# Two heads in one generator: the chunk solves of a hybrid trunk's mixer, run pair by pair on compact 32x32 blocks

## The chip, the cores and the metric

One core of a Trainium2 chip runs the whole kernel in one launch. The metric is device time in microseconds (us), the median over runs. The engines are named as in the profile: PE (TensorE, matmuls), PEld (its weight loads), DVE (VectorE), ACT (ScalarE), POOL (GpSimd) and SP (SyncE, which issues DMAs).

## What is computed

A trunk of two layers on one sequence of 512 tokens and 1024 channels. Each layer is a gated feed-forward, a mixer and a second feed-forward, each between two RMS norms. The mixer is the place of the change:

```
proj = h @ w_in            # q, k, v, z of 4 heads of 128; beta, a; u (512 channels of S5)
q, k, v = silu(causal_dwconv(qkv));  q, k normalised per token
per head, in chunks:       # gated delta rule
    lmat   = (k * beta) k^T * decay, strictly lower
    sol    = solve(I + lmat, [v * beta | k * beta * exp(g)])
    attn   = q k^T * decay
    S, o   = recurrence over the chunks with sol, attn and the state S
y_gdn = rms_norm(o) * silu(z)
y_s5  = S5 (a diagonal state-space scan) on u, with a gated output
y     = [y_gdn | y_s5] @ w_out
```

The triangular solve is the part that the change rewrites. The kernel works with chunks of 128 tokens, so that each head has four systems of 128x128, and it computes each system's inverse X: first all diagonal blocks of 16x16 by substitution on DVE, then levels that join two inverted blocks by matmuls (16 to 32, 32 to 64, 64 to 128).

## The kernel before

Projections and feed-forwards are matmuls of 128x512 in pieces, each product as three matmuls of high and low parts (mm3, L266 to L270). For them ACT casts each weight tile to its high part wh (L225), and DVE or, for the mixer's weights, POOL takes the low part wl (L233).

The mixer of a layer is built from generators, Python functions that record instructions up to a `yield`. The loop at its end calls every active generator once a round, and beside them some steps of the main work: nine a round in `main1` (projections of head 2, of the S5 input u and of head 3, by ORDER = "2u3"; heads 0 and 1 are projected ahead), one or two in `main2` (z, the S5 gate gl, the output projection od). Of the instructions so recorded a scheduler sets each engine's order; from then on an engine runs its queue strictly in that order, and waits on semaphores at its head.

`gen_head` (L921) is the generator of one head. Four of them exist; heads 0 and 1 start with the loop, 2 and 3 when their v is there. Its steps, with the tiles that the profile names (m0h2U is tile U of head 2 in layer 0's mixer):

- tk, tq: PE transposes of k and q, with sums of squares by ACT into ss.
- pu = k k^T for four chunks (L937), U = pu x beta's factors x decay on DVE, read from PSUM (L962). ub = U x mask (L967), and a reduction over the blocks (L969) makes uc, in which each 16x16 diagonal block is one row of 16 numbers.
- pa = k^T q (L937), at = pa x decay (L973); r8, ir, sq, sp: small factors.
- The substitution: 15 steps of three DVE operations (STREAM_SHUFFLE L985, product L986, difference L987) on 128 partitions x 4 chunks x up to 15 numbers, each waiting for the one before. Heads that run at the same time take turns.
- X0: the block-diagonal 128x512 tile of the four inverses, by POOL (L991). pt: its transpose by PE (L931).
- Level 16: pp and px as whole 128x128 matmuls (L937) with a mask on DVE (L1029) and a difference (L1032). Level 32 and 64: matmuls of 32x32 and 64x64, a block pair at a time (L1010 flips a block, L1018 pp, L1024 px), with ACT copies between. tv, vb, kc, kst are made beside.
- pk, then four steps of recurrence with the state S, and after two and after four of them `finish`, which norms half of o, transposes it and multiplies with z.

`gen_s5` (from L827) makes one S5 channel after another: ut, vr, vi on PE, products L851 to L856 and L869 to L877 with scans L862 and L865 on DVE and some on POOL, y on PE, and yf, yh, yl, of which DVE makes yl (L895). The S5 gate gl in `main2` needs the yl of all four channels. In the feed-forward behind the mixer, f02i is the tile of its first matmuls.

Of the kernel before, what the change touches and what calls it, by code (L numbers as in the profile page):

```python
# [56 lines left out]
def trunk(ctx: ExitStack, tc: tile.TileContext, x_d, c, wmod, wun, vecs, wab, s5p, cst_d, out, depth=2):  # L57
# [863 lines left out]
    def gen_head(l, hd, qkv, gates, decs, zs, yk, done, nm):  # L921
        v = vec[l]
        beta, gh, gr, eg = gates
        q, k, vv = [qkv.pop((hd, i)) for i in range(3)]
# [23 lines left out]
        for c in range(4):
            ACT.activation(junk, q4(tq)[:, c], AF.Square, accum_out=ss[:, c:c + 1])
        yield  # L950
        while hd not in decs:
# [2 lines left out]
        DVE.tensor_scalar(ss, ss, EPS, None, op0=ALU.add)
        s2 = small(4, nm + "s2")
        DVE.reciprocal(s2, ss[:, 4:8])
        DVE.tensor_tensor(s2, s2, be, op=ALU.mult)
        yield
        pu = mm4("pu", k, k)
        U = slot(nm + "U")  # L960
        for c in range(4):
            DVE.scalar_tensor_tensor(q4(U)[:, c], q4(pu)[:, c], s2[:, c:c + 1], q4(dec)[:, c],  # L962
                                     op0=ALU.mult, op1=ALU.mult)
        nb = P // BASE
        bd = cst[:, C_BD:C_BD + P]
        ub = slot(nm + "ub")
        DVE.tensor_tensor(q4(ub), q4(U), rep(cst[:, C_BS:C_BS + P], 4), op=ALU.mult)  # L967
        uc = small(4 * BASE, nm + "uc")
        DVE.tensor_reduce(uc, ub.rearrange("p (c b s) -> p c s b", c=4, s=BASE), axis=mybir.AxisListType.X, op=ALU.add)  # L969
        yield  # L970
        pa = mm4("pa", k, q)
        at = slot(nm + "at")
        DVE.tensor_tensor(at, pa, dec, op=ALU.mult)  # L973
        r8 = rsqrt(ss, nm + "r8")
        ir, sq, sp = small(4, nm + "ir"), small(4, nm + "sq"), small(4, nm + "sp")
# [584 lines left out]
```

## Time and profile before

| | |
|---|---|
| median of 3 runs | 2166.43 us (2165.65 to 2166.83) |
| the profiled execution | 2169.05 us |
| its span | 2166.9 us |
| mean granted clock of TensorE | 0.971 |
| busy: PE, PEld | 2070.8 us, 1756.8 us |
| busy: DVE, ACT, POOL | 1319.2 us, 861.5 us, 538.4 us |

The span is the profiled stretch on the core; the execution's own time lies 2.2 us above it. Granted clock is a share of full speed. Times within the trace are counted from the span's start.

### The profile page before, as it was taken

The numbers are of one execution on the slowest core, as the hardware profiler recorded it, in microseconds if no ns is written. First come the engines' busy times: TensorE is split into PE (matmuls) and PEld (weight loads), VectorE is DVE, ScalarE is ACT, GpSimd is POOL, SyncE is SP. The second block draws the span as 40 slices with busy tenths as digits, with TensorE's granted clock in tenths as the row PEclk, the third lists the DMA queues.
The fourth block names the chain that finished last, engine by engine and source line by source line (L and its number), as shares of the span: only waits on it lengthen the run. The fifth ranks groups of instructions, "written<-read, shape, count | busy, mean of one in ns | idle before, by whom it ended". The sixth has DMA issues, their size and how long they took to land.

```text
span 2166.9 us, 30734 instructions
## 1 busy us (share of the span) xinstructions
PE 2070.8 (96%) x10870; PEld 1756.8 (81%) x10870; DVE 1319.2 (61%) x3500; ACT 861.5 (40%) x1924; POOL 538.4 (25%) x937
## 2 busy tenths in 40 slices
PE   7999899999789999999999999999987999999998
PEld 5778688798678888888889888888976879888886
DVE  7855658757967844555574456468489486234235
ACT  4432313565236632322363232236632565333132
POOL 3147685111431015676010000001124300000001
PEclk9999999999979999999999999999998899999999
DMA  7586666404212235556423555542132123224231
GB/s 261 178 313 191 214 195 211 137 30 151 81 54 69 78 112 168 168 191 187 156 88 117 168 163 185 184 136 79 59 127 83 45 66 111 78 87 136 78 98 49
DMA packets 109693, 286.13 MB, mean 132 GB/s; under 512 B 31154, under 2 KB 32610, under 8 KB 109540
## 3 DMA queue, kind: packets, MB, share of 16 engines
q1 hardware_dynamic: 108388, 282.39, 40.0%
q8 instruction: 85, 1.39, 0.3%
q10 hardware_dynamic: 1152, 1.79, 0.3%
q14 instruction: 68, 0.56, 0.1%
HBM read 267.72 MB, written 16.41 MB: 131 GB/s over the span
## 4 chain that ended last, share of the span: by engine, by line
PE 69%; DVE 17%; DMA 4%; issue 4%; ACT 3%; POOL 2%; SPq 0%; DVEq 0%; ACTq 0%; POOLq 0%
PE f10i L268 4%; PE f10i L269 4%; PE f10i L270 4%; PE f12i L270 3%; PE f12i L268 3%; PE f12i L269 3%; PE f02i L268 3%; PE f02i L270 3%; PE f02i L269 3%; DMA wm<-in_wmod 3%; DVE wl L233 3%; PE f00i L268 1%; PE f00i L269 1%; PE f00i L270 1%; ACT wh L225 1%
## 5 line engine op out<-in xcount | busy, mean ns | idle before, releaser
L233 DVE TENSOR_TENSOR wl<-w,wh 128x512 fp32r<-128x512 f32 x608 | 407.4, 722 | 91.4 <-ACT wh L225 90.4
L225 ACT CAST wh<-w 128x512 fp32r<-128x512 f32 x648 | 357.2, 618 | 109.5 <-DMA w<-in_wun 56.1
L145 DVE SCALAR_TENSOR_TENSOR wm<-wm,cb 128x1024 f32<-128x1024 f32 x128 | 159.4, 1246 | 228.8 <-DMA wm<-in_wmod 228.7
L268 PE MATMUL f10i<-f02ohh,wh 128*128 128x512 f32 (+1 forms) x416 | 150.4, 362 | 1.5 <-DVE f02pt L326 1.3
L269 PE MATMUL f10i<-f02ohl,wh 128*128 128x512 f32 (+1 forms) x416 | 149.4, 359 | 2.1 <-ACT f02ohl L406 2.1
L268 PE MATMUL f02i<-m0ohh,wh 128*128 128x512 f32 (+1 forms) x416 | 148.7, 360 | 1.3 <-ACT f02sg L499 0.8
L270 PE MATMUL f10i<-f02ohh,wl 128*128 128x512 f32 (+1 forms) x416 | 149.3, 359 | 0.0
L268 PE MATMUL f12i<-m1ohh,wh 128*128 128x512 f32 (+1 forms) x416 | 148.1, 358 | 0.8 <-ACT f12sg L499 0.8
L269 PE MATMUL f02i<-m0ohl,wh 128*128 128x512 f32 (+1 forms) x416 | 148.1, 357 | 0.1
L269 PE MATMUL f12i<-m1ohl,wh 128*128 128x512 f32 (+1 forms) x416 | 148.0, 357 | 0.1
L270 PE MATMUL f12i<-m1ohh,wl 128*128 128x512 f32 (+1 forms) x416 | 147.8, 357 | 0.2 <-DVE wl L233 0.2
L270 PE MATMUL f02i<-m0ohh,wl 128*128 128x512 f32 (+1 forms) x416 | 147.8, 357 | 0.2 <-DVE wl L233 0.2
L269 PE MATMUL f00i<-h0l,wh 128*128 128x512 f32 x344 | 135.7, 394 | 3.8 <-DVE h0l L1416 3.8
L270 PE MATMUL f00i<-h0h,wl 128*128 128x512 f32 x344 | 135.1, 393 | 0.0
L268 PE MATMUL f00i<-h0h,wh 128*128 128x512 f32 x344 | 132.1, 393 | 1.7 <-ACT h0h L1411 1.7
L332 POOL TENSOR_TENSOR f12pt<-f12pt,Gr 128x512 f32<-128x512 f32 x8 | 10.5, 1316 | 407.8 <-ACT scr L331 407.8
L332 POOL TENSOR_TENSOR f10pt<-f10pt,Gr 128x512 f32<-128x512 f32 x8 | 10.7, 1340 | 361.5 <-ACT scr L331 357.7
L233 POOL TENSOR_TENSOR wl<-w,wh 128x512 fp32r<-128x512 f32 x40 | 56.9, 1441 | 170.7 <-ACT wh L225 168.0
L500 DVE TENSOR_TENSOR f12sg<-f12sg,f12i 128x512 f32<-128x512 f32 (+1 forms) x26 | 15.7, 605 | 136.9 <-PE f12i L270 120.8
L269 PEld LDWEIGHTS f10i<-f02ohl,wh 128*128 128x128 f32 x416 | 79.7, 192 | 13.5 <-ACT f02ohl L406 2.4
L268 PEld LDWEIGHTS f10i<-f02ohh,wh 128*128 128x128 f32 x416 | 79.6, 191 | 13.4 <-DVE f02pt L326 1.6
L268 PEld LDWEIGHTS f02i<-m0ohh,wh 128*128 128x128 f32 x416 | 78.2, 189 | 13.2 <-ACT f02sg L499 1.0
(2799 smaller groups left out, 5463.9 us busy)
## 6 DMA issues: line engine op xcount, KB each, us to landing
w<-in_wun SPq DMA_DIRECT2D x324, 512.0 KB, 3.8
wm<-in_wmod SPq DMA_DIRECT2D x128, 512.0 KB, 4.3
wm<-in_wmod SPq DMA_DIRECT2D x32, 256.0 KB, 6.0
s5d<-zero SPq DMA_DIRECT2D x4, 1280.0 KB, 13.7
Gr<-Gd SPq DMA_DIRECT2D x12, 256.0 KB, 3.4
x<-in_x SPq DMA_DIRECT2D x4, 512.0 KB, 5.7
m0s0tb<-s5d SPq DMA_DIRECT2D x7, 256.0 KB, 4.0
m0s1tb<-s5d SPq DMA_DIRECT2D x7, 256.0 KB, 5.0
```

Of the source, the lines that this page charges most:

```text
L145: DVE.scalar_tensor_tensor(w, w, 1.0, cb, op0=ALU.mult, op1=ALU.mult, accum_out=m)
L225: ACT.copy(hi[j], raw[:, j * T:j * T + T])
L233: e.tensor_tensor(lo[j], raw[:, j * T:j * T + T], hi[j].bitcast(F32), op=ALU.subtract)
L268: PE.matmul(ps, hi, h[0][:, sl], start=start, stop=False)
L269: PE.matmul(ps, hi, h[1][:, sl], start=False, stop=False)
L270: mark["pe"] = PE.matmul(ps, lo, h[0][:, sl], start=False, stop=stop)
L332: (POOL if self.part else DVE).tensor_tensor(y, src, self.G[dh], op=ALU.mult)
L500: DVE.tensor_tensor(sg, sg, pu[:, :n], op=ALU.mult)
```

## The change

Two generators `gen_pair` take the place of the four `gen_head`: pair 0 (tiles m0g0...) holds heads 0 and 1, pair 1 (m0g1...) heads 2 and 3. What both heads do alike on small tiles is now one instruction for both:

- The substitution runs on 128 partitions x 8 systems, so a pair is one chain of 45 DVE operations (L1004 to L1006) instead of two chains.
- U is scaled by ACT out of PSUM (L977) and multiplied by the decay on DVE (L979); ACT copies its 32x32 diagonal blocks into a compact tile cu of 128x256 (L982). A mask and one addition make uc (L985, L986).
- The inverse's diagonal blocks are kept in the compact form too: xc is made by DVE (L1009) instead of X0 by POOL, and transposed by DVE within 32x32 blocks (L1015, L1032) instead of by PE.
- Level 16 is 32 matmuls of 32x32 for pp and for px (L1024, L1030), level 32 16 of each (L1042, L1049), level 64 is 8 of 64x64 (L1057 pt2, L1076, L1086). The full tile X is put together by ACT copies over POOL memsets.
- Norm factors, `finish` and the recurrence's steps go through both heads in turn. `finish` has one more yield.
- Pair 0 does tk and tq of both heads, a yield after each, before pu. Pair 1 starts when head 2's v is there, and waits for head 3's.
- The constants' masks shrink to 32 columns, and the sizes of the small buffers are set anew.

ORDER stays "2u3". The diff's core (the parts left out are factors, the recurrence and `finish`, which do the same work in turns):

```diff
-NSMALL = {1: 12, 2: 24, 4: 28, 8: 12, 4 * BASE: 6, 128: 8}
+NSMALL = {1: 12, 2: 16, 4: 16, 8: 13, 16: 6, 128: 11}
...
-    def gen_head(l, hd, qkv, gates, decs, zs, yk, done, nm):
+    def gen_pair(l, pr, qkv, gates, decs, zs, yk, done, name):
...
+        hds = (2 * pr, 2 * pr + 1)
...
+        for i in TWO:
+            while (hds[i], 2) not in qkv:
+                yield
...
+            tk = tr(k[i], nms[i] + "tk")
...
+            yield
+            tq = tr(q[i], nms[i] + "tq")
...
+            yield
...
+        cu, cx = slot(nm + "cu"), slot(nm + "cx")
+        ud, xc = [t.rearrange("p (j n) -> p j n", j=8) for t in (cu[:, :HT], cu[:, HT:])]
+        xt, pe = [t.rearrange("p (j n) -> p j n", j=8) for t in (cx[:, :HT], cx[:, HT:])]
+        for i in TWO:
+            pu = mm4(nms[i] + "pu", k[i], k[i])
+            U[i] = slot(nms[i] + "U")
+            for c in range(4):
+                ACT.activation(q4(U[i])[:, c], q4(pu)[:, c], AF.Copy, scale=s2[:, 4 * i + c:4 * i + c + 1])
...
+            DVE.tensor_tensor(U[i], U[i], dec[i], op=ALU.mult)
+            for g in range(4):
+                gs = slice(32 * g, 32 * g + 32)
+                ACT.copy(ud[gs, 4 * i:4 * i + 4], q4(U[i])[gs, :, gs])
...
+        uc = small(8 * BASE, nm + "uc")
+        DVE.tensor_tensor(pe, ud, rep(cst[:, C_BS:C_BS + 32], 8), op=ALU.mult)
+        DVE.tensor_tensor(e8(uc, BASE), pe[:, :, 0:BASE], pe[:, :, BASE:32], op=ALU.add)
+        yield
...
+        for i in TWO:
+            pa = mm4(nms[i] + "pa", k[i], q[i])
+            at[i] = slot(nms[i] + "at")
+            DVE.tensor_tensor(at[i], pa, dec[i], op=ALU.mult)
...
         for s in range(BASE - 1, 0, -1):
-            b3, s3 = [e3(t)[:, :, s:] for t in (xb, xs)]
+            b3, s3 = [e8(t, BASE)[:, :, s:] for t in (xb, xs)]
             DVE.stream_shuffle(s3, b3, mask=[BASE * (i // BASE) + s for i in range(32)])
-            DVE.tensor_tensor(s3, s3, e3(uc)[:, :, s:s + 1].to_broadcast([P, 4, BASE - s]), op=ALU.mult)
+            DVE.tensor_tensor(s3, s3, e8(uc, BASE)[:, :, s:s + 1].to_broadcast([P, 8, BASE - s]), op=ALU.mult)
             DVE.tensor_tensor(b3, b3, s3, op=ALU.subtract)
...
-        X = slot(nm + "X0")
-        POOL.tensor_tensor(X.rearrange("p (c b s) -> p c b s", c=4, s=BASE),
...
+        DVE.tensor_tensor(xc.rearrange("p j (b s) -> p j b s", s=BASE),
...
+        G4 = [slice(32 * g, 32 * g + 32) for g in range(4)]
+        DVE.transpose(cx[:, :HT], cu[:, HT:])
         yield
...
+        pp = bg8("pp0", 32)
+        for j in range(8):
+            for g in G4:
+                PE.matmul(pp[g, j], ud[g, j], xt[g, j], start=True, stop=True)
+        DVE.tensor_tensor(pe, pp, rep(cst[:, C_LV:C_LV + 32], 8), op=ALU.mult)
         yield
...
+        px = bg8("px0", 32)
+        for j in range(8):
+            for g in G4:
+                PE.matmul(px[g, j], pe[g, j], xc[g, j], start=True, stop=True)
+        DVE.tensor_tensor(xc, xc, px, op=ALU.subtract)
+        DVE.transpose(cx[:, :HT], cu[:, HT:])
+        X4 = slot(nm + "X4")
+        x4 = X4.rearrange("p (j n) -> p j n", j=8)
+        POOL.memset(X4, 0.0)
+        for n, g in enumerate(G4):
+            ACT.copy(x4[g, :, 32 * (n % 2):32 * (n % 2) + 32], xc[g])
         yield
+        pp = bg8("pp1", 32)
+        for j in range(8):
+            for lo, hi in ((0, 1), (2, 3)):
+                PE.matmul(pp[G4[hi], j], q4(U[j // 4])[G4[lo], j % 4, G4[hi]], xt[G4[lo], j], start=True, stop=True)
+        for hi in (1, 3):
+            ACT.copy(pe[G4[hi]], pp[G4[hi]])
+        yield
+        px = bg8("px1", 32)
+        for j in range(8):
+            for lo, hi in ((0, 1), (2, 3)):
+                PE.matmul(px[G4[lo], j], pe[G4[hi], j], xc[G4[hi], j], start=True, stop=True)
...
+        pt = bg8("pt2", 64)
+        for j in range(8):
+            PE.matmul(pt[H2[0], j], x4[H2[0], j], ident[H2[0], H2[0]], start=True, stop=True)
...
-        mk = lambda hd: gen_head(l, hd, qkv, gates, decs, zs, yk, fin, f"{name}h{hd}")
+        mk = lambda pr: gen_pair(l, pr, qkv, gates, decs, zs, yk, fin, name)
         m1, m2 = main1(), main2()
-        active = [gen_decay(gates, decs, name, wait), mk(0), mk(1), *s5]
+        active = [gen_decay(gates, decs, name, wait), mk(0), *s5]
         m = m1
-        started = 2
+        started = 1
...
-            while started < 4 and (started, 2) in qkv:
+            while started < 2 and (2 * started, 2) in qkv:
                 active.append(mk(started))
```

On PE, u's last third (m0u) and the beginning of z. In the order before, pu of heads 0 and 1 stand within u:

```order
L1214 MATMUL m0u_5176<-wl_1_4971,f00ohh_4054 128x512
L937 MATMUL m0h0pu<-m0c_4447 128x128 x4
L937 MATMUL m0h1pu<-m0c_4574 128x128 x4
L931 MATMUL m0h2tq<-cst,m0c_4917 128x128 x4
L1212 MATMUL m0u_5176<-wh_0_5045,f00ohh_4056 128x512
```


Now they stand behind the first 24 matmuls of z, just ahead of S5's first matmuls:

```order
L267 MATMUL m0z_5417<-f00ohl_4059,wh_1_5238 128x512
L268 MATMUL m0z_5417<-f00ohh_4058,wl_1_5242 128x512
L941 MATMUL m0h0pu<-m0c_4447 128x128 x4
L941 MATMUL m0h1pu<-m0c_4574 128x128 x4
L845 MATMUL m0s0vr<-m0s0U,m0s0tb_5315 128x128 x4
L847 MATMUL m0s0vi<-m0s0U,m0s0tb_5317 128x128 x4
L845 MATMUL m0s1vr<-m0s1U,m0s1tb_5330 128x128 x4
L266 MATMUL m0z_5554<-f00ohh_4044,wh_0_5278 128x512
```


On DVE, the substitution. Before, the operations of heads 0 and 1 take turns:

```order
L985 STREAM_SHUFFLE m0h0xs<-m0h0xb 128x4x2
L987 TENSOR_TENSOR m0h1xb<-m0h1xb,m0h1xs 128x4
L986 TENSOR_TENSOR m0h0xs<-m0h0xs,m0h0uc 128x4x2
L985 STREAM_SHUFFLE m0h1xs<-m0h1xb 128x4x2
L987 TENSOR_TENSOR m0h0xb<-m0h0xb,m0h0xs 128x4x2
L986 TENSOR_TENSOR m0h1xs<-m0h1xs,m0h1uc 128x4x2
L985 STREAM_SHUFFLE m0h0xs<-m0h0xb 128x4x3
```


Now, behind the S5 results yl, pair 1's operations on eight systems follow one another:

```order
L1004 STREAM_SHUFFLE m0g1xs<-m0g1xb 128x8x8
L893 TENSOR_TENSOR m0s2yl<-m0s2yf,m0s2yh 128x512
L1005 TENSOR_TENSOR m0g1xs<-m0g1xs,m0g1uc 128x8x8
L1006 TENSOR_TENSOR m0g1xb<-m0g1xb,m0g1xs 128x8x8
L1004 STREAM_SHUFFLE m0g1xs<-m0g1xb 128x8x9
L1005 TENSOR_TENSOR m0g1xs<-m0g1xs,m0g1uc 128x8x9
L1006 TENSOR_TENSOR m0g1xb<-m0g1xb,m0g1xs 128x8x9
L1004 STREAM_SHUFFLE m0g1xs<-m0g1xb 128x8x10
```


On PE, behind the gate matmuls gl. Before, the small matmuls of heads 0 and 1 in level 32 (L1018, L1024) and a level-16 product of head 2 stand there:

```order
L270 MATMUL m0gl_6644<-m0s2yh,wl_0_5913 128x512
L1018 MATMUL m0h0pp_6260<-m0h0T_6006,m0h0U 32x32 x4
L1018 MATMUL m0h1pp_6272<-m0h1T_6013,m0h1U 32x32 x4
L937 MATMUL m0h2px_6292<-m0h2X_6112,m0h2pe_6243 128x128 x3
L1018 MATMUL m0h0pp_6260<-m0h0T_6006,m0h0U 32x32 x4
L1018 MATMUL m0h1pp_6272<-m0h1T_6013,m0h1U 32x32 x4
L937 MATMUL m0h2px_6292<-m0h2X_6112,m0h2pe_6243 128x128
L1024 MATMUL m0h0px_6312<-m0h0X_5930,m0h0pe_6261 32x32 x4
```


Now the first 32 small matmuls of pair 1 stand there, and pair 0's level 64 (pt2, tile m0g0pt) and both heads' tv behind them:

```order
L268 MATMUL m0gl_6536<-m0s2yh,wl_0_5799 128x512
L1024 MATMUL m0g1pp_6181<-m0g1cx,m0g1cu 32x32 x32
L1057 MATMUL m0g0pt_6221<-cst,m0g0X_6086 64x64 x8
L935 MATMUL m0h0tv<-cst,m0c_4453 128x128 x4
L935 MATMUL m0h1tv<-cst,m0c_4580 128x128 x4
L1030 MATMUL m0g1px_6264<-m0g1cu,m0g1cx 32x32 x32
L1076 MATMUL m0g0pp_6307<-m0g0Z,m0h0U 64x64 x4
```


Over the whole program, PE goes from 10048 to 10144 instructions, DVE from 3235 to 2859, ACT from 1729 to 1785, POOL from 942 to 946; SP stays at 730.

## Rows read from the trace of the kernel before

**Rows 1.** The page, busy time, share of the span and instructions of each engine.
```profile
PE 2070.8 (96%) x10870; PEld 1756.8 (81%) x10870; DVE 1319.2 (61%) x3500; ACT 861.5 (40%) x1924; POOL 538.4 (25%) x937
```

**Rows 2.** Windows: length, busy us (x instructions) of each engine, PEclk, DMA share, GB/s.
```profile
550.00:560.00 10.00, 6.54 (x35) 6.04 (x36) 9.20 (x15) 1.79 (x6) 3.16 (x3) 0.83 0.04 11
...
600.00:610.00 10.00, 5.89 (x25) 4.21 (x25) 9.78 (x65) 3.89 (x6) 1.28 (x1) 0.80 0.07 28
...
620.00:630.00 10.00, 7.03 (x63) 5.46 (x62) 7.12 (x17) 5.39 (x18) 5.46 (x6) 0.82 0.40 131
630.00:640.00 10.00, 10.00 (x97) 8.39 (x98) 4.09 (x8) 3.87 (x12) 5.75 (x6) 0.50 0.01 2
640.00:650.00 10.00, 10.00 (x79) 9.28 (x77) 1.47 (x4) 2.87 (x5) 2.08 (x2) 0.65 0.01 2
650.00:660.00 10.00, 9.96 (x104) 8.34 (x102) 2.14 (x5) 8.58 (x20) 2.51 (x2) 1.00 0.11 27
```

**Rows 3.** Chain that ended last, 600 to 700 and layer 1's place: start, us, what.
```profile
610.53 1.71 PE m0h0px L937 x8
...
630.58 0.56 PE m0h0px L1024 x8
...
656.52 0.36 PE m0h3pp L1018 x8
...
1668.98 1.72 PE m1h0px L937 x8
```

**Rows 4.** Timeline of PE, 515 to 541: start, us, engine, line, operation, tiles, idle before.
```profile
515.24 1.05 PE L937 MATMUL m0h0pu<-m0c 128*128 128x128 f32 x8
516.13 1.06 PE L937 MATMUL m0h1pu<-m0c 128*128 128x128 f32 x8
...
534.48 0.66 PE L841 MATMUL m0s2ut<-cst,m0utc 128*128 128x128 f32 x4 [1.70 <-DVE m0h0at L973]
...
540.43 0.39 PE L268 MATMUL m0z<-f00ohh,wh 128*128 128x512 f32 x1
540.65 0.39 PE L269 MATMUL m0z<-f00ohl,wh 128*128 128x512 f32 x1
```

**Rows 5.** Groups by line and form, 500 to 700: busy us, mean ns, idle before.
```profile
L962 DVE SCALAR_TENSOR_TENSOR m0h2U<-m0h2pu,m0h2s,m0h2dec 128x128 f32<-128x128 f32 x4 | 1.1, 346 | 2.0 <-PE m0h2pa L937 2.0
L969 DVE TENSOR_REDUCE m0h2uc<-m0h2ub 128x64 f32<-128x512 f32 x1 | 1.0, 1016 | 0.0
L1040 ACT ACTIVATE m0h0vb<-m0h0tv,m0h0ir 128x128 f32<-128x128 f32 x4 | 1.1, 346 | 0.0
L1018 PE MATMUL m0h3pp<-m0h3T,m0h3U 32*32 32x32 f32 x16 | 0.9, 194 | 0.0
```

**Rows 6.** Timeline of DVE, 543 to 616, columns as in rows 4.
```profile
543.30 1.20 DVE L987 TENSOR_TENSOR m0h1xb<-m0h1xb,m0h1xs 128x44 f32<-128x44 f32 x1
...
552.02 0.68 DVE L851 TENSOR_TENSOR m0s0t<-m0s0tb,m0s0vr 128x512 f32<-128x512 f32 x1
...
604.25 0.68 DVE L895 TENSOR_TENSOR m0s0yl<-m0s0yf,m0s0yh 128x512 fp32r<-128x512 f32 x1
604.86 0.21 DVE L987 TENSOR_TENSOR m0h2xb<-m0h2xb,m0h2xs 128x60 f32<-128x60 f32 x1
604.99 0.18 DVE L987 TENSOR_TENSOR m0h3xb<-m0h3xb,m0h3xs 128x28 f32<-128x28 f32 x1
...
615.07 0.22 DVE L985 STREAM_SHUFFLE m0h3xs<-m0h3xb 128x52 f32<-128x52 f32 x1
615.32 0.21 DVE L986 TENSOR_TENSOR m0h3xs<-m0h3xs,m0h3uc 128x52 f32<-128x52 f32 x1
```

**Rows 7.** Timeline of POOL, 541 to 596, columns as in rows 4.
```profile
541.90 2.54 POOL L233 TENSOR_TENSOR wl<-w,wh 128x512 fp32r<-128x512 f32 x2 [0.89 <-ACT wh L225]
...
594.69 1.26 POOL L991 TENSOR_TENSOR m0h0X<-cst,m0h0xb 128x512 f32<-128x512 f32 x1
```

**Rows 8.** Instructions on tile f02i: count, ns min/median/max, first and last start, forms.
```profile
L268 PE MATMUL f02i<-m0ohh,wh x416: 277/389/499, 734.0 to 1065.2; 128*128 128x512 f32 x96, 128*128 128x256 f32 x43
```

More of the change, by code (lines that the diff above doesn't have):

```diff
@@ L954, in gen_head @@
[L954 to L975, printed above, removed]
@@ new lines, in gen_pair @@
+        kc, vb = [None, None], [None, None]
+        for i in TWO:
+            tv = tr(vv[i], nms[i] + "tv")
+            vb[i] = slot(nms[i] + "vb")
+            for c in range(4):
+                ACT.activation(q4(vb[i])[:, c], q4(tv)[:, c], AF.Copy, scale=ir[:, 4 * i + c:4 * i + c + 1])
+            vv[i] = tv = None
+        yield
+        pp = bg8("pp2", 64)
+        for j in range(8):
+            PE.matmul(pp[H2[1], j], q4(U[j // 4])[H2[0], j % 4, H2[1]], z8[H2[0], j], start=True, stop=True)
@@ new lines, in gen_pair @@
+        ACT.copy(Z[H2[1]], pp[H2[1]].rearrange("p j n -> p (j n)"))
+        for i in TWO:
+            kc[i] = slot(nms[i] + "kc")
+            hs = 4 * hds[i]
+            POOL.tensor_tensor(q4(kc[i]), q4(kt[i]), col(eg[:, hs:hs + 4], P), op=ALU.mult)
+            POOL.tensor_tensor(q4(kt[i]), q4(kt[i]), col(eg[:, 16 + hs:20 + hs], P), op=ALU.mult)
+        yield
+        px = bg8("px2", 64)
+        for j in range(8):
+            PE.matmul(px[H2[0], j], z8[H2[1], j], x4[H2[1], j], start=True, stop=True)
@@ new lines, in gen_pair @@
+        for i in TWO:
+            DVE.tensor_scalar(q4(X[i])[H2[0], :, H2[1]], px[H2[0], 4 * i:4 * i + 4], -1.0, None, op0=ALU.mult)
+        U = Z = z8 = X4 = x4 = pp = px = pt = None
+        yield
+        for i in TWO:
+            pk = mm4(nms[i] + "pk", kc[i], X[i])
+            ACT.activation(kc[i], pk, AF.Copy, scale=-1.0)
+            pk = None
+        o = [slot(n + "o") for n in nms]
+        om = small(8, nm + "om")
+        S = [None, None]
+        yield
+        m2 = lambda t, n: t.rearrange("p (i c) -> p i c", i=2)[:, :, 2 * n:2 * n + 2]
@@ new lines, in gen_pair, with finish @@
+        r2 = lambda t: t.rearrange("p (i c) -> p i c", i=2)
+        yt = {}
+        def finish(n):
+            cs, sl = slice(2 * n, 2 * n + 2), HALF[n]
+            mv = small(4, nm + f"mv{n}")
+            DVE.tensor_tensor(r2(mv), m2(sp, n), m2(om, n), op=ALU.mult)
+            DVE.tensor_scalar(mv, mv, EPS, None, op0=ALU.add)
+            rr = rsqrt(mv, nm + f"rr{n}")
+            DVE.tensor_tensor(r2(rr), m2(sq, n), r2(rr), op=ALU.mult)
+            for i in TWO:
+                o2 = q4(o[i])[:, cs]
+                DVE.tensor_tensor(o2, o2, col(rr[:, 2 * i:2 * i + 2], P), op=ALU.mult)
+            yield
+            for i, hd in enumerate(hds):
+                while zs[hd] is None:
+                    yield
+                pt = bgps(nms[i] + f"pon{n}")
+                for c in range(2):
+                    PE.transpose(pt[:, c * P:c * P + P], q4(o[i])[:, 2 * n + c], ident)
+                if n == 0:
+                    yt[i] = (zs[hd], slot(nms[i] + "yh", F32R), slot(nms[i] + "yl", F32R))
+                y, yh, yl = [t[:, sl] for t in yt[i]]
+                DVE.scalar_tensor_tensor(y, pt[:, :HT], v[:, V_GNW:V_GNW + 1], y, op0=ALU.mult, op1=ALU.mult)
+                ACT.copy(yh, y)
+                DVE.tensor_tensor(yl, y, yh.bitcast(F32), op=ALU.subtract)
+                yk[hd] = yt[i][1:]
+                done[n].add(hd)
+                if i == 0:
+                    yield
```

224 lines of the change are left out of this document (93 added, 131 removed).

## The prediction

> **What bounds the kernel now.** I read the page's busy line first: PE is busy in 96% of the span and DVE in 61% [rows 1]. So nearly all of this kernel is matmuls in a row, and work taken from DVE, ACT or POOL is worth only the time in which PE stands still, or runs at less than its full clock, because of that work. Next I read the windows around the mixer of layer 0 [rows 2]. There PE has gaps: it is idle for 3.46, 4.11 and 2.97 us in the three windows 550 to 560, 600 to 610 and 620 to 630 (10.5 us), and in the same windows DVE is busy 9.20, 9.78 and 7.12 us of 10. After them PE is busy without a gap, but at a granted clock of 0.50 and 0.65, which is largely the lower of its two levels, 1.2 GHz. From 650 on it is 1.00 again. The chain of waits [rows 3] passes in this stretch from DVE's work to the heads' small matmuls (m0h0px at 630.58), and from there on it is PE. So the mixer is DVE-bound from about 550 to 629, and what a faster DVE is worth is read at one point: **when PE comes to the first small matmuls of the last solve, and what it still has to do from there**. The chain has the same place in layer 1, at 1668.98 for 610.53 in layer 0, 1058.45 us later: a gain in one layer is had twice.
>
> **Start of the solves.** In the order before, PE computes the Gram blocks pu of heads 0 and 1 in the midst of u, and their pa after them. A head's list of four products, eight passes on PE, takes 0.89 us (515.24 to 516.13) [rows 4]. In the changed order pu stands behind the first 24 matmuls of z, pa later still. That takes 4 x 0.89 us from ahead of z, and the wait of 1.70 us at 534.48, which ends with DVE's m0h0at, goes as well: 5.3 us. So z starts at 540.43 - 5.3 = 535.1. Its 24 matmuls follow at 0.23 us (540.43 to 540.65, rounded up), 5.5 us, and two pu 1.8: done at 542.4. Then U: eight ACT scalings and eight ACT copies of 32x32 blocks. A scaling is 1.1 us for four (L1040 [rows 5]), so 2.2 us, and I take the copies at the same price, 2.2. DVE's last multiplication by the decay, mask and add take 1.2, handoffs about 0.5. S5's first product, which stands behind them on DVE, starts at 548.5, where it was 552.02 before [rows 6]: -3.5 us.
>
> **From there to the first S5 result** (m0s0yl) DVE needed 52.2 us, up to 604.25 [rows 6]. By the two orders, with DVE instructions counted between these two points:
> - Solve. Before: 64 operations of heads 2 and 3 (the solves of heads 0 and 1 were over), in turns, so that one covers the latency of the other: 0.13 us from one to the next (604.86 to 604.99), a little less for narrow ones, 7.7 us in all. After: all 45 operations of pair 0 and 17 of pair 1. Each is twice as wide, but a pair is one dependent chain. What a lone chain costs is seen in head 3, 0.25 us a step (615.07 to 615.32, at 52 elements a partition); for up to 120 elements I take 0.275. With other work between (37 of pair 0's) I take 0.15, just above the 0.13 of a narrow operation in turns. So 37 x 0.15 + 8 x 0.275 + 17 x 0.13 = 10.0: **+2.2 us**.
> - U: 8 scalings from PSUM at 0.28 (1.1 for four in L962 [rows 5]) become 2 products of 128x512 at 0.61 (604.25 to 604.86): -1.0.
> - The two reductions to uc (1.02 each, L969 [rows 5]) and two mask products (0.61) become one mask product of half the width and two small additions (0.75 together): -2.5.
> - Reciprocal roots and small factors, 24 operations of 4 or 8 columns that I take at 0.06, half of the 0.13 above, become half as many: -0.7. Two more products at: +1.2.
> - X0, now xc, comes from POOL to DVE, with one 32x32-block transpose of 128x256. The trace has no transpose; by the nearest DVE rows it lies between a shuffle (0.22 [rows 6]) and a reduction that reads 512 columns (1.02). I take 0.42, near the shuffle, whose work is most like it, and 0.35 for xc: +0.8.
> - DVE's idle 2.0 us ahead of m0h2U (L962 [rows 5]) goes, since the new U waits on nothing that is late: -2.0.
>
> Sum -2.0: m0s0yl at 548.5 + 50.2 = 598.7, which is 5.5 us earlier.
>
> **From there to pair 1's first small matmuls.** Behind m0s0yl the changed order has on DVE 28 solve operations of pair 1, 20 of them with nothing between (5.5 us) and 8 covered (1.2); three yl (1.8); nine 128x512 operations of S5 channel 3 (5.5) and eight scans at 0.34 (2.7; by the 128x128 rows); and seven 128x256 operations of the pairs at 0.35 (2.5). To that come 2.0 us for DVE standing behind POOL: while POOL made wl for 2.54 us from 541.90 [rows 7], a solve operation took 1.20 us (543.30 [rows 6]) where others take 0.21. Sum 21: xc and its transpose at 619.7. On PE, m0g1pp stands at the head of the queue there, and everything of pair 0 from pt2 on stands behind it.
>
> **What PE has to do from there** to f02i, the first matmul of the feed-forward behind the mixer: 213 matmuls of 128x512, 96 of 128x128, 52 transposes, 48 of 64x64 and 96 of 32x32. Before, from m0h0px (630.58) on: 213, 104, 48, 48 and 64. At 0.11 for a 128x128 (0.89 for eight), 0.16 for a transpose (0.66 for four, 534.48 [rows 4]) and 0.045 for a 32x32 (656.52: 0.36 for eight [rows 3]) after has 1.2 us more, so the same point lay at 629.4 before. 619.7 against 629.4 is **9.7 us a layer, 19.4 us in all**, if PE runs on as it did. The profiled execution took 2169.05 us, the median of the runs is 2166.43, 2.6 lower. 2169.05 - 19.4 = 2149.65, and in terms of the median **2147**.
>
> **What costs nothing, and its cover.** POOL loses X0 (1.26 us a head, 594.69, where it waited behind S5's and wl [rows 7]) and gets memsets of X4 and X; bounds are nothing and the 1.27 us of such a product, over in either case before pp2 needs them. ACT gets some 9 us a layer of scalings and copies, where it is busy 18 to 54% from 550 to 650 [rows 2]; they would cost if they held up the wh casts on the same queue. The smaller constants are loaded in the beginning, beside other transfers.
>
> **The rivals.**
> - *Forecast, chance 0.50.* Gain of 6 to 13 us a layer (the priced solve and transpose terms at their bounds): 2140 to 2154.
> - *The clock holds, 0.13.* The half-clock stretch from 630 to 650 [rows 2] comes right after PE's gaps; if they shrink, the clock may stay at 1.00. That saves up to 10 x 0.50 + 10 x 0.35 = 8.5 us more a layer: 2130. For it speaks that 650 to 660 is at 1.00 behind a full stretch; against it, that DVE is full and PE still waits for it, so that gaps remain.
> - *The merged chain is bare, 0.17.* If none of the 62 solve operations is covered, all cost 0.275: 37 and 8 x 0.125 and 17 x 0.145 more, 8.1 us a layer. That leaves 1.7 a layer, 2163: no difference that can be measured, since a measurement of this kernel tells some 0.2%, 4.3 us, from no change. For it speaks the lone pitch of head 3; against it, that the order sets S5's products between 37 of them.
> - *Slower: the row groups in turns, 0.14.* Level 16 and 32 are now lists in which each matmul of 32x32 reads another group of 32 partitions than the one before and writes into the same bank: 96 a pair, 192 a layer. Before, lists of eight went four by four through a group and took 0.045 us a matmul at full clock [rows 3], overlapped; a single one lasts 0.194 on average (L1018 [rows 5]). If a change of group keeps two from overlapping, each costs 0.194: 192 x 0.149 = 28.6 us a layer, of which about 6 lie in gaps. Minus the 9.7: +12.9 a layer, 2192. It decides from 0.127 us a matmul. Against it speaks that the lists before change group once or twice without a gap to be seen.
>
> The Trainium skill, page "TensorEngine Tiling (Array Packing)", section "Restrictions and Gotchas", gives the rule behind this rival: "Different row tiles cannot access same PSUM bank simultaneously". By it the new lists would run one matmul at a time; no list of the trace changes group at every matmul, so no run here shows it yet.
>
> **How the numbers follow.** The chances above leave 0.06 for sums that are off in other ways. Faster by over 0.2% (below 2162): the forecast, the held clock, a small part of the bare chain: 0.63. Within 0.2%: most of the bare chain and a little else, 0.16. Slower: row groups and some mishaps, 0.21. The forecast's own range is 2140 to 2154; from the held clock to beyond the bare chain, without the row groups' 2192, it is 2129 to 2176.
>
> **What would show it.** Right: m0s0yl at about 599 where it was 604, m0g1pp at about 620, f02i at about 724 where it was 734.0 [rows 8], and 0.15 us from one covered solve operation to the next. Wrong: lists of m0g0pp at over 0.1 us a matmul; solve operations that stand in a row at 0.275 through the S5 stretch; a z that doesn't start earlier than 540; or a gain at m0g1pp that is lost again ahead of f02i, which would mean that another work than PE's bounds the rest, the recurrence on ACT and DVE first of all.

## The result and the profile after

The changed kernel takes 2141.91 us (median of 4 runs, 2139.82 to 2144.71), the kernel before beside it 2166.04 (2164.64 to 2166.83, 4 runs): a ratio of 0.989, interval 0.9873 to 0.9907. It is faster by 24 us, 5 more than forecast, and lies within the forecast's own 2140 to 2154. That is luck as far as the sum goes: of the 9.7 us a layer that were forecast from DVE some 4 are there, and more than the rest came from PE, for which the forecast had nothing. The first view is the page's busy line.

```profile
PE 2034.7 (95%) x11094; PEld 1725.4 (81%) x11094; DVE 1272.1 (59%) x3064; ACT 882.3 (41%) x1980; POOL 529.5 (25%) x941
```

Against before [rows 1], DVE has 47 us less to do and PE 36, ACT 21 more. PE's are the ones that a full PE sees. To see where, I divided the mixer of each layer at four points: the first z, m0s0yl, the small matmuls at which the prediction read the gain (before: m0h0px at 630.5 [rows 3], head 0's, 3.3 us behind the end of PE's last wait of over 2 us; after: m0g1pp, the first of the last solve), and the first output matmul od; it begins with the first projection and ends with f02i. The windows of before, layer 0, with the columns of rows 2:

```profile
425.00:540.40 115.40, 110.01 (x668) 101.85 (x667) 78.05 (x265) 73.95 (x194) 19.32 (x16) 0.97 0.26 85
540.40:604.30 63.90, 50.15 (x298) 43.22 (x296) 61.74 (x233) 19.43 (x41) 27.14 (x24) 0.92 0.31 101
604.30:630.50 26.20, 21.31 (x150) 17.32 (x150) 20.20 (x58) 7.51 (x21) 8.36 (x7) 0.79 0.16 51
630.50:668.10 37.60, 37.56 (x340) 32.49 (x339) 11.65 (x24) 20.42 (x52) 12.32 (x12) 0.78 0.05 16
668.10:734.00 65.90, 63.88 (x357) 53.00 (x356) 55.95 (x229) 42.76 (x123) 5.86 (x5) 1.00 0.25 81
```

The same five of the changed kernel, and of its layer 1 the third and fourth, where the layers differ:

```profile
421.00:531.00 110.00, 106.43 (x636) 98.38 (x635) 63.68 (x159) 73.81 (x195) 19.22 (x16) 0.97 0.29 94
531.00:596.40 65.40, 52.06 (x370) 46.19 (x369) 55.17 (x169) 23.97 (x67) 22.40 (x21) 0.87 0.27 85
596.40:620.40 24.00, 14.81 (x181) 10.11 (x176) 22.49 (x64) 8.87 (x15) 7.75 (x8) 0.76 0.21 68
620.40:648.50 28.10, 26.46 (x386) 22.87 (x386) 5.85 (x14) 21.88 (x49) 12.65 (x16) 0.91 0.06 20
648.50:715.10 66.60, 64.43 (x363) 53.74 (x363) 53.95 (x182) 45.35 (x132) 5.05 (x4) 1.00 0.26 80
...
1641.40:1665.90 24.50, 14.28 (x171) 9.90 (x170) 23.45 (x64) 8.48 (x15) 8.63 (x11) 0.74 0.19 63
1665.90:1696.60 30.70, 29.03 (x386) 25.39 (x386) 5.83 (x14) 21.89 (x49) 11.43 (x13) 0.82 0.07 19
```

The mixer begins at 421.0 where it began at 425.0: the first feed-forward, which the change doesn't touch, ended earlier in this execution. Over the runs of all kernels below this point lies between 419.4 and 426.2, so I count from it. The mixer of layer 0 then goes from 309.0 to 294.1 us, that of layer 1 from 308.6 to 297.8. Of layer 0's 14.9 us, 5.4 are won ahead of z, 1.5 lost before the first S5 result, 2.2 won in the third stage, 9.5 in the fourth, and 0.7 lost in the last. The fourth is the largest, and the least foreseen: PE is full in it before, and idle for 1.6 us of it after. Multiplied by the granted clock it is 37.6 x 0.78 = 29.3 us at full clock before and 28.1 x 0.91 = 25.6 after (25.2 in layer 1): 4 us are work that PE no longer has, and 5.8 (in layer 1 2.8) a clock that comes back to the upper level sooner. The beginning of the stage shows that, first before, then after:

```profile
630.50:646.50 16.00, 16.00 (x132) 14.33 (x132) 4.59 (x8) 4.71 (x14) 7.83 (x8) 0.50 0.01 3
```

```profile
620.40:625.40 5.00, 5.00 (x104) 4.49 (x108) 0.42 (x1) 1.95 (x5) 4.88 (x8) 0.50 0.01 3
625.40:630.40 5.00, 5.00 (x128) 4.77 (x122) 0.87 (x2) 4.90 (x15) 0.66 (x1) 0.97 0.02 3
```

The granted clock is 0.50, the lower level, for at least 16 us of the stage before, and for 5 after.

PE's timeline of the changed kernel, start, us, engine, line, operation, tiles, idle before, shows the points that the prediction named:

```profile
531.04 0.39 PE L266 MATMUL m0z<-f00ohh,wh 128*128 128x512 f32 x1
...
536.48 1.05 PE L941 MATMUL m0h0pu<-m0c 128*128 128x128 f32 x8
...
595.71 0.75 PE L1024 MATMUL m0g0pp<-m0g0cx,m0g0cu 32*32 32x32 f32 x64
...
620.38 1.08 PE L1024 MATMUL m0g1pp<-m0g1cx,m0g1cu 32*32 32x32 f32 x64 [4.32 <-DVE m0g1cx L1015]
```

z starts 110.0 us into the mixer (forecast 535.1 - 425.0 = 110.1). m0g1pp waits at the head of PE's queue for DVE, as foreseen, but at 199.4 us into the mixer, not 194.7. And a list of 32 products of 32x32, which the trace counts as 64 passes, two to a product, takes 0.75 us at full clock, 1.08 at the lower: 0.012 to 0.017 us a pass, where the lists of before took 0.045 [rows 3].

### The profile page after: what moved, and what is told of

The parts are those of the page before. It is cut to its first block, busy times and chain, and to the rows that moved or that the text cites. A ratio compares the mean times of both kernels' runs of the same rounds, so it can differ in the third digit from the quotient of the medians.

```text
span 2138.7 us, 30816 instructions
## 1 busy us (share of the span) xinstructions
PE 2034.7 (95%) x11094; PEld 1725.4 (81%) x11094; DVE 1272.1 (59%) x3064; ACT 882.3 (41%) x1980; POOL 529.5 (25%) x941
## 5 line engine op out<-in xcount | busy, mean ns | idle before, releaser
L231 DVE TENSOR_TENSOR wl<-w,wh 128x512 fp32r<-128x512 f32 x608 | 412.3, 731 | 111.6 <-ACT wh L223 110.4
L231 POOL TENSOR_TENSOR wl<-w,wh 128x512 fp32r<-128x512 f32 x40 | 52.3, 1328 | 170.0 <-ACT wh L223 157.4
```

Of the source, the lines that this page charges most:

```text
L231: e.tensor_tensor(lo[j], raw[:, j * T:j * T + T], hi[j].bitcast(F32), op=ALU.subtract)
```

## The experiments

Each is compared with 2141.91 us, the changed kernel, or 2166, the kernel before, whose median lay between 2165.4 and 2167.3 in the four groups of runs. The changed kernel was not run again beside them, so that differences from it of less than some 5 us say little.

**1 and 2: where pu stands, in either form.** The heads with pu late, and the pair with pu early, complete a table of two by two.

```diff
@@ kernel before, gen_head @@
         yield
+        if hd < 2:
+            yield
+            yield
         pu = mm4("pu", k, k)
@@ changed kernel, gen_pair, behind tk and behind tq @@
-            yield
+            if pr or i:
+                yield
```

> The kernel before, with two more yields ahead of pu in the generators of heads 0 and 1 alone, so that their pu and pa go behind the first 24 matmuls of z as in the change; heads stay single. Theory A (the place of pu is worth its 5 us a layer by itself): z starts 5 us earlier in each layer and the time falls by about 10 us, to 2156. Theory B (the place pays only with the merged substitution): the 90 narrow operations of heads 0 and 1, about 12 us at 0.13, move from DVE's time ahead of S5 into the stretch that DVE bounds; 5 us of PE are won and 6 to 12 lost a layer: 2168 to 2180.

> The changed kernel with two yields of pair 0 left out, so that pu and pa of heads 0 and 1 stand within u again, as before the change; the pair form stays. Theory A (the place of pu is worth 5 us a layer by itself): z starts 5 us later in each layer, and the time is about 2152. Theory B (the solves are what counts): pair 0's 45 substitution operations are done ahead of S5, where DVE has time, so the stretch from z to the first S5 result loses 6 to 8 us, more than z loses: 2136 to 2142.

Measured: 2191.47 us (2188.53 to 2196.39; ratio to before 1.012, 1.0102 to 1.0138), and 2146.52 (2138.51 to 2149.16; ratio 0.9915, 0.9898 to 0.9932). So theory B holds for the first, beyond its range: late pu costs single heads 26 us. In the pair it costs nothing that these runs show. Run 2 lies between its two theories, and the 4.6 us that early pu is slower lie within the spread of its runs, of which the profiled one is the fastest. The first four stages of the heads with late pu, layer 0, with PE's two waits for POOL in the third, and then all five of the pair with early pu:

```profile
422.70:532.40 109.70, 106.48 (x637) 98.44 (x636) 60.26 (x153) 73.98 (x194) 18.04 (x16) 0.97 0.29 96
532.40:598.40 66.00, 52.87 (x307) 45.82 (x305) 60.42 (x203) 15.44 (x36) 24.09 (x22) 0.87 0.27 88
598.40:644.50 46.10, 31.06 (x221) 26.34 (x221) 37.01 (x201) 14.52 (x37) 15.06 (x14) 0.77 0.09 30
644.50:675.30 30.80, 30.80 (x285) 26.35 (x284) 8.26 (x19) 16.27 (x35) 7.76 (x8) 0.84 0.07 18
```

```profile
611.55 1.11 PE L931 MATMUL m0h1pt<-cst,m0h1X 128*128 128x128 f32 x4 [6.40 <-POOL m0h1X L994]
...
637.90 1.11 PE L931 MATMUL m0h3pt<-cst,m0h3X 128*128 128x128 f32 x4 [2.19 <-POOL m0h3X L994]
```

```profile
419.40:537.00 117.60, 111.64 (x669) 102.09 (x668) 71.75 (x210) 78.21 (x211) 18.12 (x16) 0.97 0.24 76
537.00:597.70 60.70, 48.27 (x400) 43.01 (x399) 52.90 (x128) 19.36 (x51) 22.50 (x22) 0.89 0.33 116
597.70:622.00 24.30, 16.95 (x151) 13.02 (x150) 23.05 (x53) 14.56 (x30) 11.15 (x12) 0.86 0.21 69
622.00:649.90 27.90, 26.76 (x369) 23.46 (x370) 8.20 (x20) 19.20 (x47) 8.76 (x10) 0.88 0.08 21
649.90:713.20 63.30, 61.80 (x340) 51.19 (x338) 50.62 (x177) 42.02 (x119) 5.01 (x4) 1.00 0.25 83
```

With late pu both forms come to m0s0yl at the same time, 175.7 and 175.4 us into the mixer. From there to the next point (m0h0px again in the heads) the heads need 46.1 us with 201 DVE instructions, the pair 24.0 with 64. PE has other work left at these two points, but the third and fourth stage together, up to od, are 76.9 us for 52.1. 8.6 of the heads' 46.1 us are PE's waits for X0, which POOL makes in this form. With early pu the pair's z starts 7.6 us later than with late pu, its S5 stretch is 4.7 shorter and its last stage 3.3, and the end is the same, 293.8 us against 294.1 (298.3 against 297.8 in layer 1). The 5 us ahead of z are no gain by themselves: what is won there is lost again behind it, in layer 0 first as DVE work in the S5 stretch.

**3: the order of the small matmuls.**

```diff
-        for j in range(8):
-            for g in G4:
+        for g in G4:
+            for j in range(8):
                 PE.matmul(pp[g, j], ud[g, j], xt[g, j], start=True, stop=True)
```

and the same in px0, pp1 and px1.

> The changed kernel with the loops of level 16 and 32 turned round: all matmuls of one group of 32 partitions, then those of the next, the same 192 matmuls a layer. Theory A (groups in turns run beside one another: 64 passes take 0.6 us in the trace of the change): a pass costs the 0.045 us of the lists before, a list of 64 passes 2.9 us, and the four such lists and four of 32 passes cost 9 to 13 us more a layer on PE, of which half lies in PE's gaps: 2150 to 2158. Theory B (small matmuls overlap in any order): 2142.

Measured: 2153.45 us (2148.64 to 2155.11; ratio to before 0.9939, 0.9922 to 0.9956), 11.5 slower than the change: theory A. The same two lists as above on PE's timeline, and the fourth stage:

```profile
599.70 1.88 PE L1024 MATMUL m0g0pp<-m0g0cx,m0g0cu 32*32 32x32 f32 x64
...
625.29 3.03 PE L1024 MATMUL m0g1pp<-m0g1cx,m0g1cu 32*32 32x32 f32 x64 [4.55 <-DVE m0g1cx L1015]
```

```profile
625.30:659.90 34.60, 33.30 (x386) 29.71 (x386) 5.81 (x14) 22.03 (x49) 11.58 (x13) 0.79 0.06 17
```

0.75 becomes 1.88 us, 1.08 becomes 3.03. The fourth stage goes from 28.1 to 34.6 us (in layer 1 from 30.7 to 34.6), of which 34.6 x 0.79 - 25.6 = 1.7 is work at full clock and the rest the clock, which stays at the lower level for longer: 0.79 in both layers, about as in the kernel before. Up to m0g1pp nothing changes, 199.5 us into the mixer for 199.4. Groups in turns are worth 11.5 of the change's 24 us, but most of that is clock, and run 12 below, with groups in turns, has one layer at 0.78 as well.

**4, 7 and 8: work that POOL does beside a full DVE.** Run 4 puts the three POOL operations of each S5 channel on DVE in the changed kernel, run 7 the same in the kernel before, run 8 also the low parts wl of the mixer's weights.

```diff
-            POOL.tensor_tensor(t[2], t[2], t[3], op=ALU.subtract)
+            DVE.tensor_tensor(t[2], t[2], t[3], op=ALU.subtract)
...
-            POOL.tensor_tensor(g[3], ei, wr, op=ALU.mult)
+            DVE.tensor_tensor(g[3], ei, wr, op=ALU.mult)
...
-            POOL.tensor_tensor(q4(si)[:, :, 1:], q4(g[2])[:, :, :P - 1], q4(g[3])[:, :, :P - 1], op=ALU.add)
+            DVE.tensor_tensor(q4(si)[:, :, 1:], q4(g[2])[:, :, :P - 1], q4(g[3])[:, :, :P - 1], op=ALU.add)
@@ run 8, beside these @@
-                e = POOL if 16 <= n < 26 else DVE
+                e = DVE
```

> The changed kernel with the three 128x512 operations of each S5 channel that POOL makes put on DVE, 12 a layer. Theory A (DVE stands still while POOL works: in the trace of the change operations of 0.2 us take 1.2 beside POOL): each costs DVE 0.6 and frees it of about 1.0, so DVE's stretch becomes 3 to 5 us shorter a layer: 2132 to 2137. Theory B (POOL's work is mostly beside DVE's): DVE has 7.2 us more a layer, and the time is 2150 to 2156.

> The kernel before with the same 12 S5 operations a layer put from POOL to DVE as in the last run of the first four. Theory A (DVE stands still beside POOL whatever form the heads have): it gains as much as the changed kernel did, 12 us: 2154. Theory B (the gain needs the late substitution of the pair form, whose narrow operations fall beside POOL's): less than 5 us, 2161 to 2168.

> The changed kernel with S5's products on DVE, and the low parts wl of the mixer's weights, 20 of 1.3 us a layer on POOL, on DVE too. Theory A (each POOL operation beside a full DVE costs DVE more than doing it): another 3 to 6 us a layer: 2118 to 2125. Theory B (most of these lie where DVE has time, or where POOL's hold costs nothing that counts): DVE gets 14 us a layer more in its full stretch: 2135 to 2150.

Measured: run 4 2130.07 us (2127.42 to 2130.88; ratio to before 0.9832, 0.9818 to 0.9847); run 7 2164.32 (2162.33 to 2166.96; ratio 0.9989, 0.9979 to 0.9999); run 8 2119.68 (2118.02 to 2120.98; ratio 0.9785, 0.977 to 0.9799). Run 8 is the fastest kernel of all. Theory A holds for 8 and, with 2 us more gain than its range, for 4; theory B holds for 7. POOL's and DVE's timelines of the changed kernel show the mechanism; a group of four scans on DVE is one row:

```profile
560.29 2.63 POOL L231 TENSOR_TENSOR wl<-w,wh 128x512 fp32r<-128x512 f32 x2 [6.43 <-PE m0z L268]
...
607.24 1.27 POOL L855 TENSOR_TENSOR m0s3t<-m0s3t,m0s3t 128x512 f32<-128x512 f32 x1 [16.03 <-DVE m0s3t L852]
608.46 2.97 POOL L231 TENSOR_TENSOR wl<-w,wh 128x512 fp32r<-128x512 f32 x2
```

```profile
559.15 1.34 DVE L863 TENSOR_TENSOR_SCAN m0s1t<-r,m0s1t 128x128 f32<-128x128 f32 x4
560.41 3.44 DVE L860 TENSOR_TENSOR_SCAN m0s2t<-r,m0s2t 128x128 f32<-128x128 f32 x4
...
600.30 0.22 DVE L1005 TENSOR_TENSOR m0g1xs<-m0g1xs,m0g1uc 128x64 f32<-128x64 f32 x1
600.56 0.23 DVE L1006 TENSOR_TENSOR m0g1xb<-m0g1xb,m0g1xs 128x64 f32<-128x64 f32 x1
...
607.34 1.71 DVE L854 TENSOR_TENSOR m0s3t<-m0s3t,m0s3t 128x512 f32<-128x512 f32 x1
609.33 0.96 DVE L1006 TENSOR_TENSOR m0g1xb<-m0g1xb,m0g1xs 128x104 f32<-128x104 f32 x1
610.22 2.44 DVE L860 TENSOR_TENSOR_SCAN m0s3t<-r,m0s3t 128x128 f32<-128x128 f32 x4
```

Four scans take 1.34 us at 559.15 and 3.44 while POOL makes wl at 560.29; at 610.22 they take 2.44, and L1006, which takes 0.23 on 64 elements at 600.56, takes 0.96 on 104. The Trainium skill, page "SBUF — State Buffer", section "SBUF: two separate sides", states the rule: the shared port pair is an exclusive lock, and of POOL and a DVE operation with two inputs in SBUF, beside a POOL operation that reads SBUF, "whichever [...] starts first gets the pair for the whole instruction". The trace agrees: L854 starts at 607.34 beside POOL's L855, which ends at 608.51, and ends at 609.05, 0.5 us behind it and 1.71 after its start, where such an operation takes 0.68 alone (554.34). DVE's busy time over stages two and three shows what that is worth, first the changed kernel, then run 4, which has twelve more operations in these stages:

```profile
531.00:620.40 89.40, 66.87 (x544) 56.30 (x544) 77.66 (x232) 32.84 (x81) 30.15 (x29) 0.84 0.25 81
```

```profile
531.90:615.20 83.30, 65.99 (x544) 55.33 (x543) 72.31 (x244) 32.79 (x81) 12.75 (x21) 0.86 0.27 88
```

DVE is busy 5.4 us less with more to do. In the kernel before it goes from 81.94 (540.4 to 630.5) to 81.45 us in run 7: there the moved work and the time freed cancel. The DVE timelines say why they don't in the pair form. I counted in layer 0's second and third stage every DVE operation that lasts over 0.4 us longer than its form does otherwise, and added up what is too long: 16.5 us in the kernel before, 9.8 in run 7, 14.9 in the change, 5.3 in run 4, none in run 8. So 12 moved operations of 0.6 us, 7.2 in all, take 6.7 us of POOL's hold away from the heads, and 9.6 from the pair. That is 2.4 of the 5.4 us. The other 3 lie for the most part in the chain: of the pair's 90 solve operations in these stages 26 have only their chain's next one behind them, which starts 0.27 us later, and in run 4, where moved operations stand between them, 9; in the heads it is 16 in either run. Why wl's hold, which stays in runs 4 and 7, costs the heads more was not tried.

**5, 6, 10 and 12: the change's DVE parts one by one.** Run 5 makes the substitution in two chains of four systems, run 6 makes xc on POOL, run 10 makes U on DVE from PSUM and adds a product and a reduction a head as dead work, run 12 does the block transposes by PE and ACT.

```diff
@@ run 5 @@
-            b3, s3 = [e8(t, BASE)[:, :, s:] for t in (xb, xs)]
+            bs = [[e8(t, BASE)[:, 4 * h:4 * h + 4, s:] for t in (xb, xs)] for h in TWO]
+            for b3, s3 in bs:
...
@@ run 6 @@
-        DVE.tensor_tensor(xc.rearrange("p j (b s) -> p j b s", s=BASE),
+        POOL.tensor_tensor(xc.rearrange("p j (b s) -> p j b s", s=BASE),
@@ run 10 @@
-                ACT.activation(q4(U[i])[:, c], q4(pu)[:, c], AF.Copy, scale=s2[:, 4 * i + c:4 * i + c + 1])
+                DVE.scalar_tensor_tensor(q4(U[i])[:, c], q4(pu)[:, c], s2[:, 4 * i + c:4 * i + c + 1], q4(dec[i])[:, c],
+                                         op0=ALU.mult, op1=ALU.mult)
...
-            DVE.tensor_tensor(U[i], U[i], dec[i], op=ALU.mult)
+            DVE.tensor_tensor(ub, U[i], dec[i], op=ALU.mult)
...
+            DVE.tensor_reduce(ur[:, :4 * BASE], ub.rearrange("p (c b s) -> p c s b", c=4, s=BASE), axis=mybir.AxisListType.X, op=ALU.add)
@@ run 12 @@
-        DVE.transpose(cx[:, :HT], cu[:, HT:])
+        for j in range(8):
+            for g in G4:
+                PE.matmul(pt[g, j], xc[g, j], ident[g, g], start=True, stop=True)
+        ACT.copy(xt, pt)
```

> The changed kernel, with the substitution of a pair as two chains of four systems each that take turns, 90 operations a pair instead of 45; all else is as in the change. Theory A (the merged substitution is what makes the late pu bearable): the covered steps cost 0.12 to 0.13 us more each, some 50 a layer, the lone ones nothing, so 6 us a layer more: 2150 to 2156. Theory B (the merging is worth nothing, the gain lies in the compact levels alone): 2142, within 4 us.

> The changed kernel with xc, the inverse's block-diagonal start, on POOL again instead of DVE. Theory A (only the product's own time moves): DVE saves 0.4 us a pair, the handoff to POOL and back costs 0.5 to 1: 2142 to 2146. Theory B (POOL's queue was what held X0 back before, by up to 45 us): xc stands behind wl and S5's products, and each pair's levels start some us later: 2148 to 2156.

> The changed kernel, with the old form's DVE work on U put back: U from PSUM by four DVE operations a head instead of ACT's scaling, and one product of 128x512 and one reduction a head into tiles that nobody reads, 2 us a head on DVE, 4.5 of 8 us a layer for heads 2 and 3 in the stretch that DVE bounds. Theory A (DVE's own work there counts in full): 4 to 8 us a layer, 2150 to 2158. Theory B (the gain lies on PE alone): 2142 to 2146.

> The changed kernel with the two block transposes of a pair done as before the change, by PE (32 matmuls of 32x32 with the identity) and a copy by ACT, instead of one DVE instruction. Theory A (the change gains by fewer handoffs in the chain of the levels: each transpose by PE waits in PE's queue, then for ACT): 1.5 to 2.5 us a transpose, of which two of four a layer lie where PE waits for them: 4 to 6 us a layer, 2150 to 2154. Theory B (the lists are short and PE waits anyway, DVE is freed of 0.4 us each): 2140 to 2145.

Measured: 2138.46 us (2133.75 to 2142.25), 2141.19 (2138.37 to 2144.59), 2135.44 (2133.68 to 2136.24) and 2146.94 (2143.92 to 2150.31). Run 5 is within theory B, run 6 0.8 us below theory A's range and far below B's, run 10 below both, run 12 between the two. Neither the merged chain nor the place of xc is worth anything that these runs show, and U's way over ACT, if anything, costs. Only the transposes may be worth some, 5 us. These differences have to be taken with care, since the clock in the fourth stage moves as much. Of the layers' two fourth stages, run 10 has 28.1 and 28.3 us at a clock of 0.90 and 0.89, the change 28.1 and 30.7 at 0.91 and 0.82, run 12 28.5 and 32.2 at 0.91 and 0.78. In run 10 against the change 2.4 of the 4.2 us by which its mixers are shorter are that.

**9: the PE work of the old level 16 put back.**

```diff
+        for i in TWO:
+            mm4(nms[i] + "ft", U[i], cx)
+            mm4(nms[i] + "fp", U[i], cx)
         pp = bg8("pp0", 32)
...
+        for i in TWO:
+            mm4(nms[i] + "fx", U[i], cx)
         px = bg8("px0", 32)
```

> The changed kernel, with the PE work of the old level 16 put back beside the new: for each head two lists of four 128x128 products ahead of pp0 and one ahead of px0, on tiles that are there, into banks that nobody reads; 96 instructions a layer. Theory A (the compact levels gain by the PE time that they leave out at the point where PE is waited for): 12 lists of 0.9 to 1.7 us a layer, 11 to 18 us on PE, of which half lies in front of the gaps of pair 0: 6 to 10 us a layer, 2154 to 2162, about all of the rest of the gain. Theory B (PE has gaps enough there, and busy lists hold the clock up): 2142 to 2148.

Measured: 2144.83 us (2144.13 to 2147.33; ratio to before 0.9903, 0.9888 to 0.9917): 3 us, theory B. The third and fourth stage of its layer 0:

```profile
596.80:625.60 28.80, 23.53 (x316) 19.86 (x318) 23.54 (x64) 8.93 (x15) 12.41 (x15) 0.88 0.17 56
625.60:652.30 26.70, 25.77 (x403) 22.74 (x402) 5.81 (x14) 21.93 (x49) 7.64 (x9) 1.00 0.07 21
```

The lists cost the third stage 4.8 us (in layer 1 3.5), and the fourth gives 1.4 of it back (in layer 1 4.0, from 30.7), because the clock is 1.00 from its first microsecond.

**11: run 8 with the two chains of run 5.**

> The changed kernel with S5's products and the mixer's wl on DVE (2119.7 when run alone) and the substitution in two chains that take turns (3 us faster than the change when run alone). Theory A (both add up): 2116. Theory B (with wl and S5's products on DVE it has no time for 90 operations a pair): 2122 to 2128.

Measured: 2123.30 us (2121.34 to 2126.25; ratio 0.9798, 0.9782 to 0.9814), 3.6 slower than run 8: the time of theory B, but not clearly its reason. In layer 0 its S5 stretch is 59.4 us where run 8 has 57.5, its third stage 23.4 for 24.6, and its fourth 30.8 at a clock of 0.81 for 28.0 at 0.91: up to the fourth stage the 90 narrow operations cost 0.7, the clock the rest.

## Why the prediction was right, point by point

- *Bound of the mixer, and the point at which its gain is read*: right. PE waits 4.32 us for DVE ahead of m0g1pp, and is nearly full behind it. But the total came out by luck: 9.7 us a layer were forecast at this point and nothing behind it, and 5.0 and 3.6 came at it, 9.9 and 7.2 behind it.
- *Start of the solves*: right to 0.2 us. S5's first product starts at 544.25, 123.3 us into the mixer; forecast 123.5. But runs 1 and 2 show that this term is no gain of its own: it only says on which side of z the DVE work lies.
- *DVE from there to m0s0yl, -2.0*: wrong. It takes 52.1 us as before (596.37 - 544.25). The step that failed is "Sum -2.0", in three of its parts. DVE's idle time in the stretch falls from 2.0 to 0.8, not to nothing. The operations that stand behind POOL, which the sum left as they were, cost 11.0 us (11 operations) where they cost 10.4 (11) before, counted as under run 4; the group of scans at 560.41 alone is 2.1 too long. The remaining 0.4 us lie in the price of DVE's own work, which was to stay the same. Two rows of the kernel before, each 1.0 or 1.1 too long beside POOL:

```profile
583.31 1.68 DVE L877 TENSOR_TENSOR m0s0t<-m0s0t,m0s0t 128x508 f32<-128x508 f32 x1
584.91 1.22 DVE L986 TENSOR_TENSOR m0h2xs<-m0h2xs,m0h2uc 128x8 f32<-128x8 f32 x1
```

- *From m0s0yl to m0g1pp, 21 us*: 24.0. The lone substitution step was priced right: 0.275 forecast, 600.30 to 600.56 is 0.26. What was mis-sized is "2.0 us for DVE standing behind POOL". The four rows at 607.34, 609.33, 610.22 and the second scans (2.40 at 612.58) are 1.0, 0.7, 1.1 and 1.1 longer than alone: 3.9. 0.6 us in which DVE waits for ACT's yh stood in no term.
- *Behind it, "if PE runs on as it did"*: wrong by 9.9 us in layer 0 and 7.2 in layer 1, and this is where the total was saved. Two prices failed. The eight instructions of the row at 656.52 are eight passes, two to a product, so 0.045 is half the price of a product as it was; and in the new order 32 products take 0.75 us, 0.023 each, a quarter of what a product took. So PE had not 1.2 us more to do, but by time times clock 3.7 less (29.3 to 25.6). And the clock: 0.91 and 0.82 in the fourth stage for 0.78.
- *The rival "the clock holds"*, with 0.13: its mechanism is absent, its gain came in part, 5.8 and 2.8 us of 8.5. PE's gaps in the third stage did not shrink, they grew from 4.9 to 9.2 us (26.2 - 21.31 and 24.0 - 14.81), and the clock is at 0.50 at its end as it was. It comes back sooner in the fourth stage. Run 3, with the groups one after another, has 0.79 there in both layers, but run 12, with groups in turns, 0.91 and 0.78: what brings the clock back is not shown.
- *The rival "row groups in turns"*: the opposite. The Trainium skill, page "TensorEngine Tiling (Array Packing)", says under "Restrictions and Gotchas" that different row tiles cannot access one bank at a time, and under "Key Properties" that different tiles run in parallel. Here each group also writes another 32 partitions of the bank, and the lists run 2.5 times as fast in turns as group by group (0.75 against 1.88 us): the second rule is the one that this trace bears out.
- *The rival "the merged chain is bare"*: its mechanism is absent. From S5's first product to m0s0yl 53 of the 62 solve operations have another chain's or S5's operation behind them, 0.13 us later in the median, as forecast with 54 and 0.15; and run 5, which takes the merging back, is no slower.

What adds up: to the point of equal work left on PE (629.4 before), the mixers win 5.0 us in layer 0 (199.4 for 204.4) and 3.6 in layer 1, behind it 9.9 and 7.2, 25.7 in the two profiled executions. Of the 17 us behind the point, 10.4 are the groups in turns by the mixers of run 3 (11.5 by its median). The 7 that are left there were not tried alone; work that PE no longer has is the likeliest part of them, since even with the groups one after another the fourth stage is 27.3 us at full clock for 29.3 before. The 9 us ahead of the point come from the pair form as a whole: with pu late it is what parts 52.1 from 76.9 us in the third and fourth stage. Taking back the chain, xc, U's way or the old lists, one at a time, doesn't bring them back, and the transposes bring back some 5 at most, which the runs hardly tell from nothing. Which of the rest carries them, two heads in step with half the handoffs or the compact masks, was not tried alone and stays open.

## What to carry to other kernels

Small matmuls that use one 32-partition group each are issued with the groups in turns, each into its own partitions of the bank: the same 64 passes take 0.75 us instead of 1.88. Before work is moved to POOL to spare DVE, look at DVE's durations beside it: here 12 operations and 20 weight products a layer were dearer on POOL than on a DVE that was already full, by 22 us in all; in the kernel before, moving the same 12 operations gained 2. And a stage in which PE is full is read as time times granted clock, or a few us of clock pass for the effect of the edit.

## What the runs showed of the hardware that was not expected

Lists of 32x32 products that take four groups of partitions in turns need 0.012 us a pass at full clock even into one bank, against 0.029 group by group. The granted clock can repay work: run 9 has 96 more instructions a layer on PE, keeps a mean clock of 0.978 where the change has 0.971, and is 3 us slower, though its lists had been priced at 11 or more a layer; its third stages are 8.3 us longer, its fourth, at 1.00, 5.4 shorter. And POOL's hold on DVE stretches scans as well, from 1.34 to 3.44 us for four.
